# First layer's feed-forward output product by seven quarter products for 24 of its 32 inner tiles

## The chip, the cores and the metric

The kernel runs on one core of one Trainium2 chip. The metric is the time of one execution in microseconds; a lower time is better.

## The reference

The input x has 512 tokens of 1024 features, in float32. Two layers run one after the other, each of a mixer and a feed-forward part:

```python
h1 = layer_norm(ALPHA * x + mixer(x), ln1_g, ln1_b)          # ALPHA = 4 ** 0.25
ffn = square(relu(h1 @ w1 + b1)) @ w2 + b2                   # w1: 1024 x 4096, w2: 4096 x 1024
x = layer_norm(ALPHA * h1 + ffn, ln2_g, ln2_b)
```

The mixer of the first layer is a state-space scan beside a stick-breaking attention, that of the second layer a gated convolution over 31 tokens. The change lies in `square(...) @ w2` of the first layer.

## The kernel before

**Number format.** Each float32 operand of a product is split in two parts, hi (a cast by ScalarE) and lo (the operand minus hi, a subtraction on VectorE). A product of 128 inner rows takes three matmuls: hi x hi, hi x lo, lo x hi. This holds for weights and for activations. `gemm` (L258) issues them with 128x128 weights as the stationary operand and 512 or 256 tokens as the moving one, so results lie with features on partitions and tokens along the row.

**Stages** of the first layer, by the names in the trace: `tla` is the mixer's output product with its second half, `fl` the first six hidden tiles ("lead", computed while the layer norm `a` of the second half of the tokens runs), `f` the other hidden tiles, `acf` the output product into `X` (`accum`), `tlb` the output product of the last eight inner tiles, which runs half by half of the tokens into layer norm `b`. Then `pl`, `pv`, `pg` are the first product of the convolution. The 4096 inner features are 32 tiles of 128. The first layer takes them in four blocks of eight: eight `f` tiles, then 8 feature tiles x 8 inner tiles x 3 matmuls of `acf`; the last block's is `tlb`. So `acf` is 3 x 192 matmuls over 512 tokens.

**The second layer** takes its inner tiles in blocks of 6, 6, 6, 6 and 8, and uses Strassen's scheme in the form of Winograd (seven products of quarters in place of eight) for the first 24. The trace calls these products `s` (L1400). A block's activations are made by `pair`: two hidden tiles, each relu and square on ScalarE, then four sums of quarters on VectorE (`q`), then the split into `ah` and `al`. The weights' quarters lie in four buffers `quad`; `Weights.operand` makes the combinations in place by four subtractions (L133 to L139), and each of the seven operands is split to hi and lo (128x1536). `seven` has the activations stationary and 512 features moving, so its results lie by tokens.

**Weights** come through one list of units (`W.units`), in the order of their use. SP issues a load into a buffer `raw` (two of them), ScalarE casts it (L112), VectorE subtracts (L113), and the pair lands in a slot. `W.next()` hands out the next unit and prepares those ahead of it: five ahead over eight slots in the first layer, three ahead over four slots in the second layer's feed-forward. A slot can be filled again when what read it has ended.

**Kept weights.** 30 units of the second layer (24 of the convolution, the first six of its `w1`) are loaded and split during the first layer's feed-forward, and SP writes hi and lo back to memory (`kepth`, `keptl`, 512 KB each). POOL loads them later without a split. `keep_at` says behind which step each of them is handled.

**Memory.** Pools are stacks. `mw` has three slots, `w2` above it `raw` and five slots, `hid` at the other end the temporary tiles and the convolution's pages. When the second layer's feed-forward begins (`turn`), these pools are closed and smaller ones (slots `s1` to `s4`, `raw`, the activations `a0` to `a2`, `q`, `w` for the quads) are opened over the same bytes; a new tile waits for the old tiles under it. The order in which the engines get their instructions is made by a scheduler from dependencies and program order, so PE's matmuls need not come in program order.

Of the kernel before, what the change touches and what calls it, by code (L numbers as in the profile page):

```python
# [39 lines left out]
FFN_BLOCKS = ((8, 8, 8, 8), (6, 6, 6, 6, 8))  # L40
# [7 lines left out]
KEEP_FROM = 8  # L48
# [11 lines left out]
class Weights:  # L60


    def __init__(self, tc, ahead):
        self.tc, self.nc, self.ahead = tc, tc.nc, ahead
        self.slots, self.units, self.raw, self.urgent, self.fence, self.hold = [], [], None, True, None, False
        self.done, self.got, self.chunk, self.ready, self.kept = 0, 0, {}, {}, {}
        self.turn, self.quads, self.base = None, {}, 0
# [19 lines left out]
    def _prep(self, n):  # L87
        nc = self.nc
        while self.done < min(n, len(self.units)):
            key, src, nk, ncol, off, width = self.units[self.done]  # L90
            if self.turn and self.done == self.turn[0]:
                self.turn[1]()
# [106 lines left out]
def kernel(ctx: ExitStack, tc: tile.TileContext, a: dict, out: bass.AP):  # L199
# [7 lines left out]
    def const(shape, name, dt=F32):  # L207
        return cst.tile(shape, dt, tag=name, name=name)
# [4 lines left out]
    X = [const([P, T], f"X{j}") for j in range(KT)]  # L213
# [49 lines left out]
    wst = ExitStack()  # L263
    wpool = wst.enter_context(tc.tile_pool(name="mw", bufs=1))
# [600 lines left out]
    wp2 = wst.enter_context(tc.tile_pool(name="w2", bufs=1))  # L865
    hst = ExitStack()
    hid = hst.enter_context(tc.tile_pool(name="hid", bufs=1, side="right"))
# [11 lines left out]
    def hpage(name, dt=F32R, w=T):  # L879
        return hid.tile([P, PAD + T + 2], dt, tag="hid", name=name, bufs=16)[:, :w]  # L880

    def tmp(name, dt=F32):
        return hid.tile([P, T], dt, tag="tmp", name=name, bufs=8)
# [9 lines left out]
    later += units_of("pw2", a["conv_w_pw2"][0], 0, 8, range(0, D, 128), 256)  # L893
    later += units_of("f1l", a["ffn_w1"][1], 0, 8, range(0, LEAD * P, 128), 256)

    kept = [k for j in range(0, 16, 4) for k in (j, j + 2, j + 1, j + 3)] + list(range(16, 24 + LEAD))
    keep_at, n = {}, 0
    for layer in range(2):
        if layer:
            units += [(("split", i), None, 8, 128, 0, 0) for i in range(24 + LEAD)]  # L900
            at_turn = len(W.units) + len(units)
        k0 = 0
        for nb in FFN_BLOCKS[layer]:
            if layer:
                units += units_of("f11", a["ffn_w1"][1], 0, 8, range(max(k0, LEAD) * P, (k0 + nb) * P, 128), 128)
                if nb == NB:
                    units += [(("quad", k0, i), None, nb // 2, T, 0, 0) for i in ORDER7]
                else:
                    for c in (0, T):
                        for k, n_ in ((0, 3), (3, 3), (6, 2)):  # L910
                            src = a["ffn_w2"][1][(k0 + k) * P : (k0 + k + n_) * P, c : c + T].rearrange("(k p) n -> p k n", p=P)
                            units.append((("f21", k0 + k, c), src, n_, T, 0, T))
                k0 += nb
                continue
            for m in range(k0, k0 + nb, 4):
                units += units_of("f10", a["ffn_w1"][0], 0, 8, range(m * P, min(m + 4, k0 + nb) * P, 128), 256)
                if m >= KEEP_FROM:
                    keep_at["f", m + 3] = kept[n : n + 2]
                    units += [later[i] for i in kept[n : n + 2]]
                    n += 2  # L920
            for j in range(0, KT, 4):
                units += units_of("f20", a["ffn_w2"][0], k0, nb, range(j * P, (j + 4) * P, 128), 256)
                if k0 + nb < 32:
                    m = 4 if j else 2
                    keep_at["a", k0, j + 3] = kept[n : n + m]
                    units += [later[i] for i in kept[n : n + m]]
                    n += m
            k0 += nb
    W.add_slots(wp2, 5)
# [150 lines left out]
    def ffn1(layer, bi, k0, nb, xs, fps, first=()):  # L1080
        hs = []
        for i in range(nb):
            m = k0 + i
            if i < len(first):
                ps = first[i]
            else:
                ps = fps(f"f{layer}{m}")
                gemm(ps, W.next(), slice(0, P), xs, 0, T)
            r = tmp(f"fr{layer}{m}")
            act(r, ps, AF.Relu, bias=pv("ffn_b1", 32 * layer + m))  # L1090
            tt(r, r, r, ALU.mult)
            pg_ = page if (i < 4) == (bi % 2 == 0) else hpage
            hh, hl = pg_(f"hh{layer}{m}"), pg_(f"hl{layer}{m}")
            split(hh, hl, r)
            hs.append((hh, hl))
            for k in keep_at.get(("f", m), ()) if layer == 0 else ():
                W.keep(k)
        return hs


# [6 lines left out]
    xs, first = tail_norm_lead(cat[4:8], "a", rb[0], ("ln1_g", 0), ("ln1_b", 0), LEAD, "fl0")  # L1107
    wdw = hid.tile([P, KT, CONV], F32, tag="wdw", name="wdw")
    mask = hid.tile([P, 32], F32, tag="mask", name="mask")

# [11 lines left out]

    k0 = 0
    for bi, nb in enumerate(FFN_BLOCKS[0]):
        if bi == 1:
            taps()
        hs = ffn1(0, bi, k0, nb, xs, nps, first if bi == 0 else ())
        if bi < len(FFN_BLOCKS[0]) - 1:
            accum(nps, hs, f"f0{bi}", 1024 // nb, bi == 0, keep=lambda j: keep_at.get(("a", k0, j), ()))
        k0 += nb  # L1130
    xs, first = tail_norm_lead(hs, "b", rb[1], ("ln2_g", 0), ("ln2_b", 0), 4, "pl")
# [188 lines left out]
    f1 = {}  # L1320

    def turn():
        wst.close()
        hst.close()
        f1.update((x, ctx.enter_context(tc.tile_pool(name=f"f1{x}", bufs=1, reuse_waits="tile"))) for x in "s1 s2 raw s3 a1 s4 a2 a0 q b w".split())
        W.slots, W.base, W.raw, W.ahead = [], W.done, f1["raw"], NSLOT - 1
        for x in ("s1", "s2", "s3", "s4"):
            W.add_slots(f1[x], 1)
        W.quad = f1["w"]
        W.load_quads(0, a["ffn_w2"][1], 0, NB)  # L1330

    W.turn = (at_turn, turn)
# [4 lines left out]
    nb_last = FFN_BLOCKS[1][-1]  # L1337
# [13 lines left out]
    R1 = [page(f"R1{t}", F32) for t in range(2)]  # L1351

    def rect(m, ps):

        r = page(f"r1{m}", F32)
        act(r, ps, AF.Relu, bias=pv("ffn_b1", 32 + m))
        return r

    def hidden(m):

        ps = stp(f"f1{m}")
        gemm(ps, W.next(), slice(0, P), xs, 0, T)
        return ps

    def split_part(hi, lo, src):
        S.copy(hi, src)
        V.tensor_sub(lo, src, hi.bitcast(F32))

    def pair(m, pss):

        q = f1["q"].tile([P, 8, H], F32, tag="q", name=f"q{m}", bufs=2)
        hi, lo = (f1[f"a{m // 2 % 3}"].tile([P, 7, H], F32R, tag=f"a{x}", name=f"a{x}{m}", bufs=1) for x in "hl")
        for e in range(2):
            r = rect(m + e, pss[e] if pss else hidden(m + e)).rearrange("p (h c) -> p h c", h=2)
            act(q[:, 1:3] if e else q[:, 0:8:7], r, AF.Square)
        split_part(hi[:, 0:3], lo[:, 0:3], q[:, 0:3])
        tt(q[:, 3], q[:, 7], q[:, 2], ALU.add)
        tt(q[:, 4], q[:, 3], q[:, 0], ALU.subtract)
        tt(q[:, 5], q[:, 0], q[:, 7], ALU.subtract)
        tt(q[:, 6], q[:, 1], q[:, 4], ALU.subtract)  # L1380
        split_part(hi[:, 3:7], lo[:, 3:7], q[:, 3:7])
        return hi, lo

    PLACE = {1: 0, 2: 1, 4: 2, 5: 3, 6: 4, 7: 5, 3: 6}

    def seven(blk, As, first):

        bank = {}
        for i in ORDER7:
            wh, wl = W.next()  # L1390
            chain = {3: 5, 7: 6, 4: 6}.get(i, i)
# [22 lines left out]
    for bi, nb in enumerate(FFN_BLOCKS[1][:-1]):  # L1414
        if bi:
            W.load_quads(k0, a["ffn_w2"][1], k0, nb)
        As = [pair(m, first[m : m + 2] if bi == 0 else None) for m in range(k0, k0 + nb, 2)]
        if bi == 0:
            residual()
        seven(k0, As, bi == 0)  # L1420
        k0 += nb
    hs = []
    for i in range(nb_last):
        if i % 3 == 0:
            hl_ = [f1[f"a{i // 3}"].tile([P, 3, T], F32R, tag=f"a{x}", name=f"b{x}{i}", bufs=1) for x in "hl"]
        r = rect(k0 + i, hidden(k0 + i))
# [88 lines left out]
```

## Time and profile before

| | |
|---|---|
| median of 3 runs (lowest, highest) | 1165.17 us (1160.34, 1166.05) |
| profiled execution | 1164.9 us |
| its span, first to last instruction | 1163.2 us |
| granted TensorE clock | 0.994 |
| PE busy | 1133.7 us, 97% |
| DVE (VectorE) busy | 820.6 us, 71% |
| ACT (ScalarE) busy | 550.0 us, 47% |

Durations below come from the profiled execution. A matmul's recorded duration overlaps with the next one's, so the rate of matmuls is read from the length of an unbroken stretch divided by its count. "DMA share" is the mean busy share of the core's 16 DMA engines.

### The profile page before, as it was taken

What the parts mean: (1) busy time and instruction counts of PE and PEld (TensorE: products, weight loads), DVE (VectorE), ACT (ScalarE), POOL (GpSimd) and SP (SyncE); (2) the same over time, 40 slices, a digit from 0 to 9 for tenths busy, and PEclk for the clock granted to TensorE, in tenths of its full rate; (3) what the DMA queues carried; (4) which work ended last, traced back from release to release, by engine and by line L of the source; (5) the groups of instructions that cost most, each with busy time, mean ns of one, the idle gap of its engine ahead of it and who ended that gap; (6) DMA issues with size and microseconds to landing.
All of it is one profiled execution on the core that took longest, in us unless ns stands there. A gap on an engine that the chain in (4) does not pass through costs nothing.

```text
span 1163.2 us, 17835 instructions
## 1 busy us (share of the span) xinstructions
PE 1133.7 (97%) x7156; PEld 948.5 (82%) x7156; DVE 820.6 (71%) x1401; ACT 550.0 (47%) x838; POOL 70.2 (6%) x125
## 2 busy tenths in 40 slices
PE   9989989999999999999999999999999999999997
PEld 7777767799888888888899867689988888888885
DVE  7999865578645645645647699988695958588337
ACT  7857759435524524523513231364673536263530
POOL 1022221000000000000002211002000000000000
PEclk9999989999999999999999999999999999999999
DMA  9621212150878778788617634156024151515211
GB/s 204 173 63 50 74 56 74 55 181 14 267 244 289 250 273 282 267 268 274 217 46 245 226 137 146 39 170 227 4 82 135 50 151 44 172 35 156 65 54 73
DMA packets 145907, 169.59 MB, mean 146 GB/s; under 512 B 13922, under 2 KB 119138, under 8 KB 145824
## 3 DMA queue, kind: packets, MB, share of 16 engines
q1 hardware_dynamic: 137024, 136.96, 37.1%
q0 software_dynamic: 8640, 31.46, 8.0%
q8 instruction: 56, 0.92, 0.3%
q14 instruction: 27, 0.22, 0.1%
q10 hardware_dynamic: 160, 0.03, 0.0%
HBM read 132.12 MB, written 35.65 MB: 144 GB/s over the span
## 4 chain that ended last, share of the span: by engine, by line
PE 78%; DMA 6%; DVE 6%; ACT 5%; issue 2%; SPq 2%; POOL 1%; DVEq 0%; ACTq 0%
PE f L258 20%; PE acf L258 10%; PE s L1400 10%; DMA raw<-in_ffn_w_dram 4%; PE tld L258 4%; PE h L1445 4%; PE tlb L258 4%; PE fl L258 3%; PE pv L258 3%; PE cw L1174 3%; PE pg L258 3%; PE tla L258 2%; PE acmo L258 2%; DVE wlo L113 2%; PE pl L258 2%
## 5 line engine op out<-in xcount | busy, mean ns | idle before, releaser
L112 ACT CAST whi<-raw 128x1024 fp32r<-128x1024 f32 (+1 forms) x150 | 156.6, 1061 | 259.1 <-PE acf L258 66.3
L113 DVE TENSOR_TENSOR wlo<-raw,whi 128x1024 fp32r<-128x1024 f32 (+1 forms) x150 | 183.6, 1236 | 122.1 <-ACT whi L112 122.1
L258 PE MATMUL f<-xah,whi 128*128 128x512 f32 x208 | 81.0, 390 | 0.0
L258 PE MATMUL f<-xal,whi 128*128 128x512 f32 x208 | 81.0, 389 | 0.0
L258 PE MATMUL f<-xah,wlo 128*128 128x512 f32 x208 | 80.9, 389 | 0.0
L258 PE MATMUL f<-xdh,whi 128*128 128x512 f32 x208 | 80.9, 389 | 0.0
L258 PE MATMUL f<-xdl,whi 128*128 128x512 f32 x208 | 80.9, 389 | 0.0
L258 PE MATMUL f<-xdh,wlo 128*128 128x512 f32 x208 | 80.9, 389 | 0.0
L258 PE MATMUL acf<-hl,whi 128*128 128x512 f32 x192 | 75.8, 395 | 0.1
L258 PE MATMUL acf<-hh,wlo 128*128 128x512 f32 x192 | 75.7, 394 | 0.0
L258 PE MATMUL acf<-hh,whi 128*128 128x512 f32 x192 | 75.3, 392 | 0.0
L1400 PE MATMUL s<-whi,al 128*128 128x512 f32 x168 | 65.0, 390 | 0.0
L1400 PE MATMUL s<-wlo,ah 128*128 128x512 f32 x168 | 64.9, 390 | 0.0
L1400 PE MATMUL s<-whi,ah 128*128 128x512 f32 x168 | 64.5, 392 | 0.0
L113 DVE TENSOR_TENSOR wlo<-quad,whi 128x1536 fp32r<-128x1536 f32 x28 | 49.1, 1754 | 7.6 <-ACT whi L112 7.5
L391 DVE SCALAR_TENSOR_TENSOR cy<-hp,wdw,cy 128x512 f32<-128x512 f32 (+1 forms) x75 | 49.5, 660 | 0.5 <-ACT cy L187 0.5
L112 ACT CAST whi<-quad 128x1536 fp32r<-128x1536 f32 x28 | 41.0, 1483 | 17.2 <-PE f L258 8.0
L97 POOL DMA_DIRECT2D whi<-kepth x30 | 16.0, 535 | 547.6 <-PE tlb L258 386.7
L258 PEld LDWEIGHTS f<-xdh,whi 128*128 128x128 f32 x208 | 39.0, 188 | 8.1
L258 PEld LDWEIGHTS f<-xah,wlo 128*128 128x128 f32 x208 | 39.0, 188 | 8.1
L258 PEld LDWEIGHTS f<-xah,whi 128*128 128x128 f32 x208 | 39.0, 188 | 8.1
L258 PEld LDWEIGHTS f<-xdl,whi 128*128 128x128 f32 x208 | 39.0, 188 | 8.1
(647 smaller groups left out, 3064.4 us busy)
## 6 DMA issues: line engine op xcount, KB each, us to landing
raw<-in_ffn_w_dram SPq DMA_DIRECT2D x35, 1024.0 KB, 6.0
kepth<-whi SPq DMA_DIRECT2D x30, 512.0 KB, 4.4
keptl<-wlo SPq DMA_DIRECT2D x30, 512.0 KB, 9.5
whi<-kepth POOLq DMA_DIRECT2D x30, 512.0 KB, 3.6
wlo<-keptl POOLq DMA_DIRECT2D x30, 512.0 KB, 4.4
raw<-in_ffn_w_dram SPq DMA_DIRECT2D x28, 512.0 KB, 4.0
raw<-in_conv_w_pw_dram SPq DMA_DIRECT2D x12, 1024.0 KB, 6.7
quad<-in_ffn_w_dram SPq DMA_DIRECT2D x16, 768.0 KB, 4.6
```

Source lines behind the costliest of these rows:

```text
L97: nc.gpsimd.dma_start(x, d)
L112: i0 = nc.scalar.copy(hi, raw).ins
L113: i1 = nc.vector.tensor_sub(lo, raw, hi.bitcast(F32)).ins
L258: ins = PE.matmul(ps[:, c0:c1], u[:, k, ksl], v[:, c0:c1], start=start and k == 0 and i == 0, stop=stop and k == n - 1 and i == 2).ins
L391: V.scalar_tensor_tensor(o, x, s, y, op0=op0, op1=op1)
L1174: PE.matmul(cps[j, c0][g][C, :], Ds[j][t // 16][R, t % 16, :], hps[j][R, t + c0 : t + c1], start=t < 4, stop=t >= n - 4, tile_position=(R. ...
L1400: PE.matmul(ps, u, v[:, p, :], start=chain == i and p == 0 and n_ == 0, stop=p == len(As) - 1 and n_ == 2, skip_group_check=True)
L1445: PE.matmul(ps, u, v, start=k == 0 and i == 0, stop=k == nb_last - 1 and i == 2)
```

## The change

The first layer takes the block sizes of the second (6, 6, 6, 6, 8) and the quarter products for its first 24 inner tiles. `quad` loads, `operand`, `pair` and the weight slots are those of the second layer, now functions of the layer. What is new is `seven_by_feature`: the weights stay stationary and the moving operand is a quarter of the activations, 256 tokens, so that results stay by features. Products 2, 5, 6, 3, 7, 4 are added to regions of `X` (which is now one tile, so that two feature tiles are added in one instruction), product 1 is gathered in two pages `R1` and added to `X` in the last block. `X` is scaled by ALPHA, and its bias added, by eight ScalarE instructions ahead of the blocks.

Pools change three times, not once: to the small ones at the end of the first layer's lead (`quarters(0)`), back to eight slots, `raw` and `hid` at the end of the fourth block (`plain`), and again to the small ones in the second layer (`quarters(1)`). The 30 kept units are loaded one by one (512 KB) where two came in one load (1024 KB), and so are the hidden weights of blocks 1 to 3. Their places: three in block 0's products, three among the hidden tiles and four among the products of each of blocks 1 to 3, six in the last block. The second layer's feed-forward computes as before.

```diff
-FFN_BLOCKS = ((8, 8, 8, 8), (6, 6, 6, 6, 8))
+FFN_BLOCKS = (6, 6, 6, 6, 8)
-KEEP_FROM = 8
+KEEP_AT = ((0, 3, 6), (0, 2, 4, 6), 6)
...
-        later += units_of("pw1", a["conv_w_pw1"][0], 0, 8, [j], 256)
-        later += units_of("pw1", a["conv_w_pw1"][0], 0, 8, [D + j], 256)
+        later += [units_of("pw1", a["conv_w_pw1"][0], 0, 8, [c], 128)[0] for c in (j, D + j)]
...
+        for bi, nb in enumerate(FFN_BLOCKS[:-1]):
+            for m in range(k0, k0 + nb, 2):
+                f1_units(m, 2)
+                if bi:
+                    kept("f", m)
+            for n, i in enumerate(ORDER7):
+                units.append((("quad", k0, i), None, nb // 2, T, 0, 0))
+                if n in KEEP_AT[bi > 0]:
+                    kept("p", k0, n)
...
+            turn_at.append(len(W.units) + len(units))
+            for m in range(k0, k0 + nb, 2):
+                units += units_of("f10", w1, 0, 8, range(m * P, (m + 2) * P, 128), 256)
+                if m - k0 < kept_last:
+                    kept("l", m)
+                    kept("l", m + 1)
+            units += units_of("f20", w2, k0, nb, range(0, D, 128), 256)
...
+    def quarters(layer):
+        def turn():
+            wst[0].close()
+            wst[0] = ExitStack()
+            f1.update((x, wst[0].enter_context(tc.tile_pool(name=f"f1{layer}{x}", bufs=1, reuse_waits="tile")))
+                      for x in "s1 s2 raw s3 a1 s4 a2 a0 q b w".split())
+            W.slots, W.base, W.raw, W.ahead = [], W.done, f1["raw"], NSLOT - 1
...
+    def plain():
+        wst[0].close()
+        wst[0] = ExitStack()
+        p1, p2 = (wst[0].enter_context(tc.tile_pool(name=x, bufs=1, reuse_waits="tile")) for x in ("mw2", "w22"))
+        hid[0] = wst[0].enter_context(tc.tile_pool(name="hid2", bufs=1, side="right", reuse_waits="tile"))
+        W.slots, W.base, W.raw, W.ahead = [], W.done, p2, 5
+        W.add_slots(p1, 3)
+        W.add_slots(p2, 5)
+
+    W.turns = {turn_at[0]: quarters(0), turn_at[1]: plain, turn_at[2]: quarters(1)}
...
-    xs, first = tail_norm_lead(cat[4:8], "a", rb[0], ("ln1_g", 0), ("ln1_b", 0), LEAD, "fl0")
+    xs, first = tail_norm_lead(cat[4:8], "a", rb[0], ("ln1_g", 0), ("ln1_b", 0), LEAD, "fl0", None, 3)
+    for j in range(KT):
+        act(X[j], X[j], AF.Identity, bias=rb[1][:, j : j + 1], scale=ALPHA)
...
+    def seven_by_feature(k0, As, first):
+        bank, opened = {}, None
+        for n, i in enumerate(ORDER7):
+            wh, wl = W.next()
+            chain = CHAIN.get(i, i)
+            for b in range(2):
+                if chain == i:
+                    bank[i, b] = nps(f"z{k0}{i}{b}")
+                ps = bank[chain, b]
+                for d in range(2):
+                    c = slice((2 * b + d) * P, (2 * b + d + 1) * P)
+                    for p, (ah, al) in enumerate(As):
+                        uh, ul = ah[:, PLACE[i]], al[:, PLACE[i]]
+                        for n_, (u, v) in enumerate(((wh, uh), (wh, ul), (wl, uh))):
...
+                            opens = chain == i and p == 0 and n_ == 0
+                            ins = PE.matmul(ps[:, d * H : (d + 1) * H], u[:, p, c], v, start=opens and d == 0,
+                                            stop=p == len(As) - 1 and n_ == 2, skip_group_check=True).ins
...
+            for b in range(2):
+                ps = bank[chain, b]
+                if i == 1:
+                    if first:
+                        S.copy(R1[b], ps)
+                    else:
+                        tt(R1[b], R1[b], ps, ALU.add)
+                else:
+                    x = region({2: 0, 5: 3, 6: 1, 3: 1, 7: 3, 4: 2}[i], b)
+                    tt(x, x, halves(ps), ALU.add)
+            if ("p", k0, n) in keep_at:
+                W.keep(keep_at["p", k0, n])
...
     for bi, nb in enumerate(FFN_BLOCKS[:-1]):
+        if bi:
+            W.load_quads(k0, a["ffn_w2"][0], k0, nb)
+        As = [pair(0, m, xs, first[m : m + 2] if bi == 0 else None) for m in range(k0, k0 + nb, 2)]
+        seven_by_feature(k0, As, bi == 0)
         k0 += nb
+    W.prep_to(W.got + 1)
...
+    hs = []
+    for i in range(FFN_BLOCKS[-1]):
+        m = k0 + i
+        ps = nps(f"f0{m}")
+        gemm(ps, W.next(), slice(0, P), xs, 0, T)
...
+        x = region(i // 2, i % 2)
+        tt(x, x, halves(R1[i % 2]), ALU.add)
...
-    xs, first = tail_norm_lead(hs, "b", rb[1], ("ln2_g", 0), ("ln2_b", 0), 4, "pl")
+    xs, first = tail_norm_lead(hs, "b", None, ("ln2_g", 0), ("ln2_b", 0), 4, "pl")
```

More of the change, by code (lines that the diff above doesn't have):

```diff
@@ L899 @@
         if layer:
             units += [(("split", i), None, 8, 128, 0, 0) for i in range(24 + LEAD)]
[L901 to L927, printed above, removed]
-            k0 += nb
@@ L1349, in residual @@
                 S.copy(X[4 * f + b], pss[b])
[L1351 to L1384, printed above, removed]
+    R1 = [page(f"R1{t}1", F32) for t in range(2)]
     def seven(blk, As, first):
```

156 lines of the change are left out of this document (98 added, 58 removed).

## The prediction

> **What bounds the kernel now.** I read the page's engine table first, then the waits of PE, the chain that ended last, and the stretches of both feed-forwards.
>
> ```profile
> span 1163.2 us, 17835 instructions
> PE 1133.7 (97%) x7156; PEld 948.5 (82%) x7156; DVE 820.6 (71%) x1401; ACT 550.0 (47%) x838; POOL 70.2 (6%) x125
> ...
> PE tlb L258 <- ACT hh L248: 0.9, 1, 0.9
> ...
> 317.88 39.71 PE acf L258 x170
> 358.19 43.75 PE f L258 x192
> 401.94 44.59 PE acf L258 x192
> 446.53 43.52 PE f L258 x192
> 490.05 32.98 PE acf L258 x143
> ...
> 614.32 11.42 PE tlb L258 x96
> 625.73 2.88 PE pl L258 x24
> ...
> 851.26 3.65 PE xt L1346 x32
> 854.92 28.71 PE s L1400 x126
> 883.63 32.64 PE f L258 x144
> 916.27 28.85 PE s L1400 x126
> ```
>
> PE works 97% of the span, and from `acf` to `tlb` its only listed wait is 0.9 us. The pieces of the chain (start, length, what) abut, so a matmul taken from here shortens the run, and any gap made here lengthens it. The rate is length by count: 0.2267 us for 512 tokens in `f` (43.52/192), 0.2322 in `acf` (117.28/505 over its three pieces), 0.1200 and 0.1190 for 256 tokens in `pl` and `tlb`. Half the tokens cost more than half.
>
> ```profile
> core 0: us, PE busy (x) PEld busy (x) DVE busy (x) ACT busy (x) POOL busy (x), PEclk, DMA share, GB/s
> 357.60:401.94 44.34, 44.34 (x201) 36.78 (x202) 27.89 (x33) 22.99 (x30) 0.00 (x0) 1.00 0.83 285
> 301.50:582.00 280.50, 279.84 (x1240) 229.26 (x1238) 152.50 (x169) 116.33 (x138) 0.00 (x0) 1.00 0.78 266
> 883.63:916.27 32.64, 32.64 (x145) 27.03 (x145) 21.20 (x23) 16.95 (x20) 0.00 (x0) 1.00 0.21 61
> 916.27:945.11 28.84, 28.84 (x127) 23.50 (x127) 24.48 (x27) 12.06 (x12) 0.00 (x0) 1.00 0.51 150
> ```
>
> Behind PE stand the DMA engines in the first layer (78% over 280.5 us, with the kept weights) and DVE in the second layer's products (24.48 of 28.84 us). The change brings both into one place.
>
> **The matmuls.** Removed: 3 x 192 = 576 of `acf`, 576 x 0.2322 = 133.8 us. Added: 4 blocks x 7 products x 4 feature tiles x 3 pairs' inner tiles x 3 = 1008 over 256 tokens, x 0.1200 = 121.0 us. So **-12.8 us**; with equal cost per column it would have been 576 x 0.125 x 0.2322 = 16.7. The `f` tiles and the last block's `tlb` keep their counts.
>
> On the full-speed rate the Trainium skill (TensorE: Matmul & The Clock Gate, Back-to-back issue gap) has N/2.4 + 2.5 ns, an estimate of 215.8 and 109.2 ns here; the two products would then differ by 14.2 us. The rows above are 5% to 10% longer, and the measurement decides.
>
> **VectorE and ScalarE.**
>
> ```profile
> L113 DVE TENSOR_TENSOR wlo<-raw,whi 128x1024 fp32r<-128x1024 f32 x146 | 176.6, 1222 | 107.2 <-ACT whi L112 107.1
> L112 ACT CAST whi<-raw 128x1024 fp32r<-128x1024 f32 x146 | 150.7, 1049 | 248.3 <-PE acf L258 66.3 <-PE s L1400 46.7 <-PE f L258 44.6
> L113 DVE TENSOR_TENSOR wlo<-quad,whi 128x1536 fp32r<-128x1536 f32 x28 | 49.1, 1754 | 7.6 <-ACT whi L112 7.5
> L112 ACT CAST whi<-quad 128x1536 fp32r<-128x1536 f32 x28 | 41.0, 1483 | 17.2 <-PE f L258 8.0 <-PE s L1400 7.3 <-PE fl L1058 1.8
> L387 DVE TENSOR_TENSOR X<-X,s 128x512 f32<-128x512 f32 x48 | 31.9, 682 | 11.9 <-PE s L1400 11.9
> L1367 DVE TENSOR_TENSOR al<-q,ah 128x768 fp32r<-128x768 f32 x12 | 11.5, 955 | 0.1
> L187 ACT ACTIVATE X<-X,rb 128x512 f32<-128x512 f32 x16 | 10.2, 719 | 0.0
> ```
>
> The second layer's rows carry every operation of a new block: four subtractions and seven splits of quads, three pairs, 14 additions of 512 columns. To them come 3 kept splits among the hidden tiles and 4 among the products, 1.222 us of DVE and 1.049 of ACT each. Products: 24.48 + 4 x 1.222 = 29.4 us of DVE in 252 x 0.1200 = 30.2 us of PE. Hidden tiles: 21.20 + 3.7 = 24.9 of 32.64. DVE fits, at 97% in the products. ACT has 12.06 + 4.2 of 30.2 there. The square moves from DVE to ACT, the eight scalings of `X` (5.8 us of ACT) are needed only at the second product's addition: nothing, while ACT has this room. The eight additions of `R1` (5.5 us of DVE) lie beside the last block's 43.5 us of `f`: nothing.
>
> **Hidden tiles to products.** At this passage the last pair isn't ready.
>
> ```profile
> 916.30 0.69 ACT L187 ACTIVATE r<-f,PV 128x512 f32<-128x512 f32 x1 [2.15 <-PE f L258]
> 917.02 0.63 ACT L187 ACTIVATE q<-r 128x512 f32<-128x512 f32 x1
> ...
> 918.93 0.83 ACT L1366 CAST ah<-q 128x768 fp32r<-128x768 f32 x1
> ```
>
> Its `ah` comes 3.5 us after `s` began, though program order wants it after six matmuls (1.4 us). PE went on with other pairs and lost 28.85 - 126 x 0.2267 = 0.3 us. In the new ring of four slots the last hidden tile's slot is next filled by product 2 (second layer: product 6): cast and subtraction, 1.483 + 1.754 = 3.2 us, against 36 x 0.12 = 4.3 us of product 1. At best 0, at worst the whole 3.2 us for each of three blocks. I take 0.3 each, **+0.9**, because the nearest rows show it; in the products themselves the slots are given back late (rivals).
>
> **First change of pools.** The leads lie in the old slots 4, 5, 6, 7, 0, 1 (units 28 to 33 over eight). `s1` covers slots 0 and half of 1, so product 1's lo waits for the last lead.
>
> ```profile
> 839.30 1.47 ACT L112 CAST whi<-quad 128x1536 fp32r<-128x1536 f32 x1 [1.80 <-PE fl L1058]
> ...
> L258 PE MATMUL fl<-xah,wlo x96: 278/283/467, 264.9 to 301.5; 128*128 128x256 f32 x96
> ```
>
> The second layer shows such a wait of a quad's cast for a lead. Here the leads end at 301.5, lo is there 1.754 us later; product 2 (slot `s3`) and the hi parts are free earlier, and two of three pairs are done. The last pair also starts at 301.5: 0.69 + 0.63 on ACT, 0.83 of cast, 0.955 on DVE, 3.1 us before its first part is there, 1.754 more if DVE takes product 1's lo first. So between 0 and 4.9 us; I take **+1.0**, since PE reorders but has no transposes (3.65 us of `xt`) to put there.
>
> **Second change (`plain`).** Counting units, the fourth block's product 4 lies in `s1`, under the new slot 0. The first `f` tile of the last block can be cast only when the last matmul of that block has ended: 1.049 for hi, 1.222 for lo. Lower end 1.05 (hi suffices for two thirds of its matmuls), upper 2.3 plus signals. **+2.3**: lo is the third matmul.
>
> **Staging in the last block.**
>
> ```profile
> raw<-in_ffn_w_dram SPq DMA_DIRECT2D x35, 1024.0 KB, 6.0
> kepth<-whi SPq DMA_DIRECT2D x30, 512.0 KB, 4.4
> keptl<-wlo SPq DMA_DIRECT2D x30, 512.0 KB, 9.5
> ...
> raw<-in_ffn_w_dram SPq DMA_DIRECT2D x28, 512.0 KB, 4.0
> ...
> ACT whi L112 <- DMA raw<-in_ffn_w_dram: 33.8, 19, 5.5
> ```
>
> Two `f` tiles (10.9 us of PE) bring one load of 1024 KB, two of 512 KB, four writes of 512 KB: 4.2 MB, three times. At the rate that 285 GB/s at a share of 0.83 gives (343) that is 12.2 us. Lower end 0 (loads begun under the products), upper 3 x (4.2 MB / 290 - 10.9) = 10.8, with 290 from 61 at 0.21. I take **+1.5**, about one of the three excesses at 343.
>
> The Trainium skill (DMA: Bandwidth & Descriptors, Anatomy of one DMA) puts a fixed 2.0 us on each transfer, so two halves of a load cost one such more. The rows agree: 2 x 4.0 against 6.0. By it the 24 split loads carry 48 us of added latency, spread over two buffers; it speaks against the change, in the second rival.
>
> **SP's queue.** A block's four quad loads wait for buffers that are freed by the casts of products 6, 3, 7 and 4; behind them stand the next hidden weights and the kept writes.
>
> ```profile
> 921.24 12.01 SPq L126 DMA_DIRECT2D quad<-in_ffn_w_dram  x4
> ...
> 935.21 23.29 SPq L78 DMA_DIRECT2D raw<-in_ffn_w_dram  x6
> ```
>
> In the second layer the queue stands 12 us on them, from 921 on, and PE, with three units prepared, shows no gap. The first layer adds two kept writes for each kept unit to the same queue; a write that is held back holds a slot. I put nothing here and leave it to the rivals. POOL's queue gets nothing new.
>
> **Third change.** The second layer's leads move by the new count to slots 6, 7, 0, 1, 2, 3: the first two quad casts, at 836.04 and 839.30 now, wait for leads 3 and 4, some 6 to 9 us later, with `xt` and DVE's queue behind. From 0 to 3.5 us (two DVE splits); **+0.5**, as `s` begins only at 854.92.
>
> None of these terms can fall below nothing: PE has no gap in `acf` and `f` that they could close.
>
> **Sum**: -12.8 + 0.9 + 1.0 + 2.3 + 1.5 + 0.5 = **-6.6 us**. The profiled execution took 1164.9 (span 1163.2 and 1.7 around), 0.3 below the median of 1165.17: forecast **1158.3**.
>
> **Rivals.**
>
> *All is hidden.* PE reorders as it does at 916, loads come ahead; only the 1.05 us of `plain` remains: -11.7, 1153.2. For it: no gap at three such passages of the second layer. Against: there the DMA share is 0.5, here above 0.8.
>
> *The transfers become the bound* (the other side). A block moves 3.1 MB of quads, 3.1 of hidden weights, 3.7 of kept loads and 7.3 of kept writes, 17.3 MB in 62.9 us: 275 GB/s, a share of 0.80 at 343, 0.95 at 290. Among the hidden tiles, if the quads fall there, 11 MB in 32.6 us want 337: at 290 it is 37.9, +5.3 in each of three blocks. With 10.8 in the last block, and half of these 16: -6.6 - 1.5 + 10.8 + 8 = +10.7, 1175.6. It decides from 14 us lost. For it: casts already wait 33.8 us for loads here. Against: PE showed no gap at 285.
>
> *The ring of four slots.* A kept unit holds its slot for 1.0 + 1.2 us of split and 9.5 of `keptl`, near 12 us or three products; product 7's lo, refilled behind the kept unit cast after product 1, comes at 4.3 + 12 + 1.8 = 18 us, wanted at 21.6. With DVE at 97% its queue can eat these 3.5 us. At 2 us a block: -6.6 - 0.9 + 8 = +0.5, 1165.4, no change.
>
> **Chances.** Forecast (1154.5 to 1161): 0.35; all hidden 0.20; slots 0.28; transfers 0.17. A measurement tells 0.5% (5.8 us) from no change, so faster means below 1159.3: 0.28 of the forecast's, the 0.20, and 0.02 of the slots': 0.50. Slower, above 1171: 0.15, of the transfers. Within: 0.35, the rest of each. The range reaches from 1152, all of the matmuls' gain, over the slots' case to 1171 and leaves out the transfers' 0.15 above that.
>
> **What would show it.** `z` matmuls 0.120 apart, 121 us in all (first step); PE gaps at the leads' end, at each passage from `f` to `z`, about 2.3 us at the end of the fourth block, and at the second layer's first `s`; the DMA share above 0.83, and `f` of the last block waiting for `whi`. It is wrong if `z` runs slower than `pl`, or if PE's waits on `whi` and `wlo` in the first layer pass 14 us.

## The result and the profile after

The changed kernel takes 1197.04 us (median of 4 runs, 1193.13 to 1200.89) against 1163.14 (1160.34 to 1166.05): a ratio of 1.0291 (95% interval 1.0237 to 1.0345). It is slower, and far outside the predicted range. The profiled execution took 1193.67 us, 28.8 more than that of before.

First the page of the changed kernel: span, engines, and the clock by slices.

```profile
span 1191.8 us, 18891 instructions
PE 1137.0 (95%) x7588; PEld 971.6 (82%) x7588; DVE 893.6 (75%) x1475; ACT 599.3 (50%) x884; POOL 66.7 (6%) x125
...
PEclk9999999999899999987999999999999999999999
```

PE's recorded busy time hardly moves, yet its share falls to 95%; the clock row, in tenths, dips in the middle of the run. Next stretches of the changed kernel, with the columns of before: the first layer's feed-forward, all behind it, and the products of one block from their first gap on.

```profile
298.47:654.43 355.96, 327.55 (x2032) 296.17 (x2031) 253.69 (x307) 167.78 (x193) 7.57 (x14) 0.95 0.69 226
654.43:1191.00 536.57, 525.23 (x3856) 439.18 (x3855) 404.00 (x652) 232.40 (x345) 24.34 (x46) 1.00 0.34 110
...
440.00:475.00 35.00, 30.87 (x243) 30.17 (x242) 30.85 (x32) 15.03 (x15) 0.00 (x0) 0.95 0.74 244
```

From the start of the last `fl` matmul to the first `pl` ("the stretch" below) it is 355.9 us, and was 324.0 (301.54 to 625.57). From there to the end both kernels take 537.6. So all of the loss lies in the stretch: PE works 327.55 of 355.96 us of it, at a mean clock of 0.95. The DMA share is 0.69 (0.74 in the same stretch of before). That is a mean, and it doesn't show whether the transfers bind at single places.

I took the stretch apart by the start times of its matmuls. An interval beyond 0.120 us (256 tokens) or 0.227 (512; `acf` at its own 0.232) is a gap; inside the windows in which the granted clock is 0.50, the excess is put to the clock.

| us | before | after |
|---|---|---|
| `acf` / `z`, at full rate | 133.4 | 121.0 |
| `f`, `tlb` and rest, at full rate | 188.5 | 188.3 |
| gaps | 2.1 | 34.7 |
| halved clock | 0 | 11.9 |

So the matmuls give 12.4 us, and gaps (+32.6) and clock (+11.9) take more than three times that. The gaps by place: end of the leads and block 0, 2.0 + 0.5 + 3.7 = 6.2; the three passages from `f` to `z` 3.5, 4.7 and 5.1, together 13.3; the end of the fourth block 10.0; the rest of the last block 3.0; small ones the remainder. The chain of the changed kernel holds the pieces between them (start, length, what, count):

```profile
337.97 21.57 PE f L259 x95
...
449.65 16.95 PE z L1200 x139
```

An unbroken piece of `z` (L1200 is `seven_by_feature`'s matmul) takes 16.95/139 = 0.122 us each, one of `f` 0.227. What PE waited for, in the waits of the changed kernel (us in total, times, longest):

```profile
PE z L1200 <- DVE wlo L113: 7.9, 4, 3.5
PE z L1200 <- ACT whi L112: 7.4, 4, 3.6
PE wd L1169 <- DMA wn<-in_conv_w_dw_dram: 5.2, 2, 4.2
PE f L259 <- ACT whi L112: 4.6, 2, 3.3
PE z L1200 <- DVE al L1107: 2.2, 4, 1.2
...
PE s L1469 <- ACT X L1451: 0.7, 1, 0.7
```

Split weights come late (L112 the cast, L113 the subtraction), and the taps' load `wn` once, at the turn. A passage in the timeline of the changed kernel (start, length, instruction, in brackets the idle time before it and its releaser):

```profile
506.02 1.06 ACT L112 CAST whi<-raw 128x1024 fp32r<-128x1024 f32 x1 [2.61 <-DMA raw<-in_conv_w_pw_dram]
506.98 0.68 ACT L187 ACTIVATE r<-f,PV 128x512 f32<-128x512 f32 x1
508.66 1.47 ACT L112 CAST whi<-quad 128x1536 fp32r<-128x1536 f32 x1 [1.00 <-DMA kepth<-whi]
510.04 1.04 ACT L1106 CAST ah<-q 128x1024 fp32r<-128x1024 f32 x1
510.99 0.63 ACT L187 ACTIVATE q<-r 128x512 f32<-128x512 f32 x1
511.52 1.46 ACT L112 CAST whi<-quad 128x1536 fp32r<-128x1536 f32 x1
...
513.03 0.38 PE L1200 MATMUL z<-ah,whi 128*128 128x256 f32 x1 [3.59 <-ACT whi L112]
```

ACT stands 2.61 us on the load of a kept unit (a convolution weight, of no use to this layer) and 1.00 us until a write-back has freed a slot. What stands behind on its in-order queue, the pair's operations and the next product's cast, is late by that, and PE waits 3.59 us. SP's issues of the changed kernel (KB each, median us to landing) show the write-backs quicker than before, when `keptl` took 9.5 us, but `keptl` still outlasts a product of 36 x 0.120 = 4.3 us:

```profile
kepth<-whi SPq DMA_DIRECT2D x30, 512.0 KB, 3.6
keptl<-wlo SPq DMA_DIRECT2D x30, 512.0 KB, 5.4
```

And the turn to the last block, in the same timeline:

```profile
545.34 0.26 SPq L1166 DMA_DIRECT2D wn<-in_conv_w_dw_dram  x1
545.70 1.02 SPq L78 DMA_DIRECT2D raw<-in_ffn_w_dram  x2
...
550.24 0.63 PE L1169 MATMUL wd<-ident,wn 31*128 31x31 f32 x4 [4.21 <-DMA wn<-in_conv_w_dw_dram]
...
553.10 2.94 ACT L112 CAST whi<-raw 128x1024 fp32r<-128x1024 f32 x3 [14.74 <-DMA raw<-in_ffn_w_dram]
554.20 0.80 PE L259 MATMUL f<-xah,whi 128*128 128x512 f32 x1 [3.33 <-ACT whi L112]
```

The taps (`wn`, L1166) go to a page of `hid2`, which exists only after the fourth block; SP waited 5.3 us with that load, until 545.3, and the hidden weights of the last block (L78) were queued behind it. PE stood 4.21 us on the taps' little transposes and 3.33 us on the first cast.

### The profile page after: what moved, and what is told of

Its sections match the earlier page's. It is cut to its first block, busy times and chain, and to the rows that moved or that the text cites. A ratio compares the mean times of both kernels' runs of the same rounds, so it can differ in the third digit from the quotient of the medians.

```text
span 1191.8 us, 18891 instructions
## 1 busy us (share of the span) xinstructions
PE 1137.0 (95%) x7588; PEld 971.6 (82%) x7588; DVE 893.6 (75%) x1475; ACT 599.3 (50%) x884; POOL 66.7 (6%) x125
## 4 chain that ended last, share of the span: by engine, by line
PE 63%; DVE 10%; DMA 8%; ACT 6%; issue 1%; SPq 0%; POOL 0%; DVEq 0%; ACTq 0%
PE f L259 15%; PE s L1469 10%; PE z L1200 7%; PE fl L259 5%; PE tld L259 4%; PE h L1514 4%; PE tlb L259 4%; DVE wlo L113 3%; DMA raw<-in_ffn_w_dram 3%; ACT whi L112 2%; PE tla L259 2%; PE pv L259 2%; PE acmo L259 2%; DMA keptl<-wlo 2%; DVE cy L393 2%; PE pl L259 2%
## 5 line engine op out<-in xcount | busy, mean ns | idle before, releaser
L113 DVE TENSOR_TENSOR wlo<-raw,whi 128x1024 fp32r<-128x1024 f32 (+1 forms) x126 | 155.2, 1240 | 129.1 <-ACT whi L112 126.9
L112 ACT CAST whi<-raw 128x1024 fp32r<-128x1024 f32 (+1 forms) x126 | 133.0, 1065 | 235.5 <-DMA raw<-in_ffn_w_dram 81.4
L112 ACT CAST whi<-quad 128x1536 fp32r<-128x1536 f32 x56 | 82.3, 1481 | 49.4 <-PE z L1200 15.9
L113 DVE TENSOR_TENSOR wlo<-quad,whi 128x1536 fp32r<-128x1536 f32 x56 | 98.0, 1754 | 10.3 <-ACT whi L112 5.8
L1200 PE MATMUL z<-ah,wlo 128*128 128x256 f32 x336 | 97.2, 294 | 7.9 <-DVE wlo L113 7.9
L1200 PE MATMUL z<-ah,whi 128*128 128x256 f32 x336 | 96.6, 295 | 7.4 <-ACT whi L112 7.4
L1200 PE MATMUL z<-al,whi 128*128 128x256 f32 x336 | 97.7, 293 | 2.2 <-DVE al L1107 2.2
L1200 PEld LDWEIGHTS z<-ah,wlo 128*128 128x128 f32 x336 | 67.2, 202 | 8.9 <-DVE wlo L113 8.9
L1200 PEld LDWEIGHTS z<-ah,whi 128*128 128x128 f32 x336 | 67.0, 203 | 8.5 <-ACT whi L112 8.2
L1200 PEld LDWEIGHTS z<-al,whi 128*128 128x128 f32 x336 | 67.2, 200 | 3.5 <-DVE al L1107 3.4
L1106 ACT CAST ah<-q 128x768 fp32r<-128x768 f32 (+1 forms) x48 | 45.1, 945 | 35.3 <-DVE q L389 33.9
L1107 DVE TENSOR_TENSOR al<-q,ah 128x768 fp32r<-128x768 f32 (+1 forms) x48 | 52.0, 1088 | 10.1 <-ACT ah L1106 10.0
L259 PEld LDWEIGHTS f<-xah,whi 128*128 128x128 f32 x208 | 40.0, 192 | 13.3 <-ACT whi L112 5.2
```

What stands on the lines that cost most here:

```text
L112: i0 = nc.scalar.copy(hi, raw).ins
L113: i1 = nc.vector.tensor_sub(lo, raw, hi.bitcast(F32)).ins
L259: ins = PE.matmul(ps[:, c0:c1], u[:, k, ksl], v[:, c0:c1], start=start and k == 0 and i == 0, stop=stop and k == n - 1 and i == 2).ins
L1200: ins = PE.matmul(ps[:, d * H : (d + 1) * H], u[:, p, c], v, start=opens and d == 0, stop=p == len(As) - 1 and n_ == 2, skip_group_check=T ...
```

## The experiments

My theory: the kept units make the passages late, above all because a slot is held until its write-back has landed; and the taps' load makes the turn late. There are two rivals: the pairs' operations and the weights' splits stand behind each other on the in-order queues of ACT and DVE, whose total work is too close to PE's, whoever holds the slots; and the transfers themselves are in each other's way.

All are judged by the stretch of one profiled execution beside the median, since the end of the leads itself varied. It lies at 297.7 to 299.4 us in the changed kernel and in e1 to e4, and at 301.5 to 308.5 in the seven kernels that have the taps ahead of it (301.5 before, 298.1 in e6_before_none). So the stretch may leave out a part of what the earlier taps cost. "Ratio" is to the kernel before on the same chip.

| | median us | ratio (95%) | stretch | gaps | halved clock |
|---|---|---|---|---|---|
| before | 1163.14 | | 324.0 | 2.1 | 0 |
| after | 1197.04 | 1.0291 (1.0237 to 1.0345) | 355.9 | 34.7 | 11.9 |
| e1_no_kept | 1173.60 | 1.0078 (1.0034 to 1.0122) | 335.6 | 19.6 | 6.7 |
| e2_no_store | 1182.44 | 1.0147 (1.0079 to 1.0215) | 342.0 | 25.4 | 6.8 |
| e4_store_elsewhere | 1188.18 | 1.0196 (1.0140 to 1.0253) | 348.5 | 31.1 | 7.8 |
| e6_before_none | 1162.54 | 0.9994 (0.9969 to 1.0019) | 323.2 | 1.3 | 0 |
| e3_taps_late | 1190.09 | 1.0213 (1.0158 to 1.0267) | 353.4 | 33.0 | 11.0 |
| e7_taps_early | 1190.17 | 1.0235 (1.0161 to 1.0309) | 346.8 | 31.0 | 7.2 |
| e5_none_early | 1164.59 | 1.0033 (1.0009 to 1.0057) | 323.4 | 12.0 | 2.9 |
| e8_kept_apart | 1193.89 | 1.0267 (1.0188 to 1.0346) | 351.0 | 31.4 | 10.9 |
| e9_pair_first | 1190.73 | 1.0235 (1.0162 to 1.0307) | 347.6 | 27.2 | 11.7 |
| e11_pool_order | 1188.80 | 1.0218 (1.0144 to 1.0292) | 343.8 | 27.1 | 7.7 |
| e12_kept_mid | 1186.24 | 1.0196 (1.0086 to 1.0306) | 342.8 | 27.9 | 5.8 |
| e11_none_ordered | 1164.84 | 1.0014 (0.9990 to 1.0039) | 320.2 | 11.7 | 0 |

**What the kept units cost.** e1_no_kept has no kept unit in the first layer; the second layer fills those slots from the unsplit weights.

```diff
-                keep_at[at] = i
-                units.append(later[i])
+                W.kept[i] = (later[i][1], later[i][1])
```

> The changed kernel without the 30 kept units in the first layer: they are neither loaded, split nor written back there, and the second layer fills those slots straight from the unsplit weights (so its results are left wrong, its matmuls the same). Theory A (a kept unit sits in the ring of four slots until its write-back has landed, and the casts of the next products stand behind it in order): the gaps at the passages from hidden tiles to products, 4 to 5 us each with the halved clock behind them, shrink to under 1 us; what remains is the change of pools at the fourth block's end. The first layer's stretch (last lead matmul to first pl) falls from 354 to about 330. Theory B (VectorE's work at the passage, quads and the last pair's sums, is too much by itself): the gaps at the passages stay at 3 us or more, stretch 345. Theory C (the transfers' rate is the bound): the stretch falls too, to about 330, and the experiments without and with the stores tell it from A.

The stretch falls by 20.3 us, the median by 23.4; 335.6 is above the 330 or so that theory A expected. The waits of e1_no_kept:

```profile
PE wd L1168 <- DMA wn<-in_conv_w_dw_dram: 5.5, 2, 4.5
PE f L259 <- ACT whi L112: 3.4, 1, 3.4
...
PE z L1199 <- DVE al L1106: 2.6, 3, 0.9
PE z L1199 <- ACT whi L112: 2.4, 3, 0.9
```

The wait on `wlo` is gone from the list's head, the passages of blocks 1 to 3 cost 1.0 us each, and the turn is as it was (4.5 and 3.4 us). So the kept units are what makes the passages late, and not the turn.

e2_no_store loads and splits the kept units and writes only the first back; e4_store_elsewhere writes as many bytes, from pages that hold other data and in four transfers a unit where there were two, so that no slot waits for a write.

```diff
 # e2
+        if self.kept:
+            self.kept[i] = self.kept[0]
+            return
 # e4
-        for x, d in zip(w, self.kept[i]):
-            self.nc.sync.dma_start(d, x.bitcast(F32))
+        for e, d in enumerate(self.kept[i]):
+            for h in range(2):
+                src = self.other[2 * h + e][0].bitcast(F32).rearrange("p (k n) -> p k n", n=P)
+                self.nc.sync.dma_start(d[:, 4 * h : 4 * h + 4, :], src)
...
+    W.other = xs
```

> The changed kernel with all 30 kept units loaded and split, but only the first written back (the second layer reads that one each time; its results are wrong for it). Slots are free after the split. Theory A: passages' gaps under 1.5 us, stretch about 335. Theory B: gaps stay at 3 to 4 us each, since the splits on VectorE stay, stretch 348 or more. Theory C: stretch about 335 too.

> The changed kernel with the same 30 kept units and as many bytes written back, but from the layer's input pages in place of the slots (results of the second layer are wrong for it), so that a slot isn't held by a write-back. Theory A: stretch about 335 to 340, as without stores. Theory C: as in the changed kernel, about 352, since the bytes are the same. Theory B: about 352.

By the stretches, holding slots costs 355.9 - 348.5 = 7.4 us, the writes themselves 6.5, loads and splits 6.4: three parts of like size. By the medians they are 8.9, 5.7 and 8.8. Each part rests on one profiled execution and two to four times of a kernel, and the changed kernel's own times spread over 7.8 us, so the order of the three isn't shown. Both measures put the held slots and the writes together (13.9 of 20.3 us by the stretches) above the loads and splits. The held slots alone are not the main part as I had it.

The gaps in the products of blocks 1 to 3, small ones included, are plainer: 14.7 us in the changed kernel, 11.9 in e4, 6.3 in e2 and 4.1 in e1. In e2 VectorE is busy 252.5 us of the stretch, as in the changed kernel (253.7), since every split is still made. So loads and splits cost 2.2 of these 10.6 us, and the rest goes with the write-backs. The DMA share ahead of a passage, twice in the changed kernel and once in e2 (a transfer counts in the stretch in which it begins, so a share can pass 1):

```profile
436.00:440.00 4.00, 4.00 (x24) 3.49 (x23) 3.35 (x4) 3.74 (x4) 0.00 (x0) 1.00 1.02 366
505.00:509.20 4.20, 4.20 (x26) 3.69 (x24) 4.00 (x5) 2.18 (x3) 0.00 (x0) 1.00 1.02 350
...
436.00:441.00 5.00, 4.40 (x32) 3.74 (x31) 4.97 (x5) 3.53 (x5) 0.00 (x0) 1.00 0.09 28
```

The mean of 0.69 hides that the DMA engines are full just there. Whether the writes act through the transfer rate or through SP's queue, these runs don't part.

e6_before_none takes the kept units out of the kernel before, whose second layer then fills from the unsplit weights.

```diff
-                    keep_at["f", m + 3] = kept[n : n + 2]
-                    units += [later[i] for i in kept[n : n + 2]]
...
-                        keep_at["a", k0, j + 3] = kept[n : n + m]
-                        units += [later[i] for i in kept[n : n + m]]
...
+    for i, u in enumerate(later):
+        W.kept[i] = (u[1][:, :, u[4] : u[4] + 128],) * 2
```

> The kernel before without the kept units in the first layer (the second layer fills from the unsplit weights, its results are left wrong). Theory A (eight slots with five ahead hide the kept units): the first layer's stretch stays at 322 to 324 us, where the changed kernel lost 20 us by them. Rival (the kept units cost the kernel before as well): 315 or less.

The first layer's stretch of e6_before_none:

```profile
298.13:621.30 323.17, 322.89 (x1599) 272.26 (x1598) 143.52 (x201) 94.66 (x124) 12.40 (x14) 1.00 0.41 101
```

The DMA share falls from 0.74 to 0.41, and PE gains nothing: the same work was free in the kernel before, with eight slots, DVE at 54% and five units ahead, and costs 20 us in the changed one. Which of these conditions made it free was not tried one by one.

**The turn.** e3_taps_late moves `taps()` behind the last hidden tile; e7_taps_early moves it ahead of the leads, into a small pool of its own.

```diff
 # e7 (e3: the three lines of wdw, mask and taps() moved behind the loop over the last block's f)
+    tp = ctx.enter_context(tc.tile_pool(name="tp", bufs=1, side="right"))
...
+    wdw = tp.tile([P, KT, CONV], F32, tag="wdw", name="wdw")
+    mask = tp.tile([P, 32], F32, tag="mask", name="mask")
...
+    taps()
     xs, first = tail_norm_lead(cat[4:8], "a", rb[0], ("ln1_g", 0), ("ln1_b", 0), LEAD, "fl0", None, 3)
...
-    wdw = hid[0].tile([P, KT, CONV], F32, tag="wdw", name="wdw")
-    mask = hid[0].tile([P, 32], F32, tag="mask", name="mask")
-    taps()
```

> The changed kernel with the convolution's taps (two loads of 62 KB, eight transposes, the mask) moved from the change of pools behind the last block's eight hidden tiles. Theory D (the taps' load waits on the queue of SP for bytes that the fourth block's products still use, and the first two loads of the last block stand behind it): those loads are issued about 5 us sooner, the gap at the end of the fourth block falls from 4.4 + 1.7 us and a clock halved for 13.7 us to about 2.5 us without or with one short halving, total 8 to 14 us less than the changed kernel. Rival: those loads wait for their own bytes, and nothing moves beyond 2 us.

> The changed kernel with the taps made ahead of the first layer's tail, nothing else. Theory S (with the queue of SP free, the last block's loads are issued some 5 us sooner, but each two tiles still bring one load of 1024 KB and two kept ones of 512 KB through two buffers): the gap at the change of pools falls to about 2 us without a halved clock; gaps of 1 to 2 us come later in the last block. Stretch 346 to 350 against 355.9. Rival (taps alone): 342 or less.

Stretches of e3_taps_late: the turn, what follows it, and a later place of the same block.

```profile
546.40:549.60 3.20, 1.10 (x6) 0.47 (x4) 2.77 (x5) 2.00 (x2) 0.00 (x0) 1.00 0.61 164
549.60:560.00 10.40, 10.32 (x45) 8.56 (x46) 3.61 (x4) 3.91 (x5) 0.00 (x0) 1.00 0.76 227
573.00:576.30 3.30, 1.29 (x5) 0.48 (x3) 0.73 (x2) 1.76 (x2) 0.00 (x0) 1.00 0.92 287
576.30:583.10 6.80, 6.27 (x16) 4.84 (x16) 3.56 (x4) 3.87 (x6) 0.00 (x0) 0.50 0.80 241
```

The gaps of the turn fall from 10.0 to 2.6 us and the clock stays full behind it, so the taps' load is the cause of the turn's gaps; but PE then stops at 573, at a DMA share of 0.92 beside the kept units of the last block, and the clock halves there. Of the 7.4 us of gaps taken away at the turn, the stretch keeps 2.5; the median is 7.0 lower, under the 8 to 14 that theory D expected. e7 keeps 9.1 in the stretch, and its median is 6.9 lower; its leads end 5.5 us later than those of the changed kernel, so its profiled execution is only 3.6 us shorter.

**Both together.** e5_none_early is e1 with the taps early.

> No kept units in the first layer (as in the earlier experiment) and the taps made ahead of the first layer's tail, so that nothing of them lies at the change of pools. Theory: what is then left of the change is the matmuls' gain, 12.8 us, minus the two changes of pools. First layer's stretch about 322 us (335.6 less 4.7 + 3.5 + 1.5 us of gaps and half of a clock halved for 13.7 us, plus 2.5 for the first cast), and about 2 us under the kernel before without kept units. Rival (the taps weren't the cause at the change of pools; the loads of the last block wait for their own bytes): 333 or more.

Its stretch, 323.4, equals that of e6_before_none, 323.2; the median is 2.05 us above. With kept units and taps gone from the picture, the gain of the matmuls is still eaten by 12.0 us of gaps and 2.9 of halved clock. The gaps of blocks 1 to 3 are 1.0 each, of the leads' end and block 0 3.9, of the turn 2.4; the rest are under 0.5 each. The stretch came near the expected 322, but the run is not the 2 us shorter than e6 that was expected with it.

**Remedies.** e8_kept_apart is e7 with two slots for the kept units alone and three for all others (to find room, one `q` buffer, not two).

```diff
+            if self.apart and key[0] in ("pw1", "pw2", "f1l"):
+                pool, s = self.apart[self.nkept % len(self.apart)]
+                self.nkept += 1
+                self.base += 1
...
+            W.apart = [] if layer else [(f1["k1"], 8), (f1["k2"], 9)]
```

> As the run before it, and kept units have two slots of their own in blocks 0 to 3, beside three for the products and hidden weights (paid for by one buffer fewer of the pairs' squares). Theory A (the ring is held by write-backs): another 7 us less, as when the write-backs came from elsewhere, stretch about 340. Rival (the order on VectorE and ScalarE: the kept units' casts now wait for their own slots and stand ahead of the products' casts): no gain or a loss, 347 or more.

It gains nothing on e7 (351.0 against 346.8). Since it also has a slot and a `q` buffer less for the rest, it doesn't clear the slots of blame; it shows only that splitting the same memory in this way is no cure.

e9_pair_first is e7 with the pairs' operations of the first layer given precedence on their engines (`high_priority` around relu, square, sums and split).

> The run with the taps made early, and the pairs' relu, squares, sums and splits of the first layer given precedence over the weights' casts where both are ready. Theory O (at the passage the last pair's cast and split stand in the engines' order behind a quad's cast that itself waits for a subtraction or a write-back): gaps in z fall from 23 to about 12 us, stretch 346.8 to about 335. Rival A (the weights themselves come late, because their slots are held): gaps move from the pair's tiles to whi and wlo of the products, stretch 344 or more.

ACT at one passage of e9_pair_first, and two rows of its waits:

```profile
442.53 1.47 ACT L112 CAST whi<-quad 128x1536 fp32r<-128x1536 f32 x1 [1.25 <-DMA kepth<-whi]
...
448.97 1.48 ACT L112 CAST whi<-quad 128x1536 fp32r<-128x1536 f32 x1 [0.87 <-DVE quad L135]
```

```profile
PE z L1208 <- ACT whi L112: 8.8, 3, 3.6
PE z L1208 <- DVE wlo L113: 5.0, 3, 2.1
```

The gaps inside `z` fall from 23.1 to 15.6 us, but 1.8 us more at its first matmul and 4.5 more of halved clock take 6.3 of these 7.5 us back, and the stretch doesn't gain (347.6 against 346.8). PE's wait in `z` for the pairs' `al` falls from 4.1 us in e7 to 0.2, while its waits for the weights' casts and splits stay (14.4 us in e7, 13.8 here).

e11_pool_order is e9 with the small pools of the first change laid so that the first quads don't lie under the last leads (order `a2 s4 raw s1 s3 a1 s2 a0 q b w`). e12_kept_mid is e9 with kept units moved out of the passages:

```diff
-KEEP_AT = ((0, 3, 6), (0, 2, 4, 6), 6)
+KEEP_AT = ((2, 4, 5), (1, 2, 3, 4, 5), 6)
...
-                if bi:
+                if bi and m < k0 + 4:
```

> As the run with pairs first, kept units present, with that order of the small pools. Theory P: 3 to 7 us less than without it, by the gap of 2 us at the leads' end and the halved clock behind it. Rival: the kept units' write-backs (the second unit of that block is one) keep the first passage late, less than 2 us.

> As the run with pairs first, and kept units moved away from the passages: two a block among the hidden tiles instead of three (none behind the last pair), five among the products 2 to 7 instead of four from product 1 on. Theory A (a kept unit ahead of a passage holds the slot of the first products): gaps at the passages fall by 2 us each, stretch 5 to 8 us less than with pairs first. Rival B (VectorE's load among the products, 24.5 + 5 x 1.2 = 30.6 us of 30.2): gaps appear inside the products, no gain or a loss.

In e11_pool_order the gap from `fl` to `z` is gone, but the gaps in all stay (27.1 us against 27.2): the 3.8 us that the stretch gains on e9 are halved clock, 7.7 us against 11.7. In e12_kept_mid the gaps in `z` fall to 13.7 and those in `f` rise to 11.0, and the sum is 27.9; its 4.8 us are halved clock too (5.8). So neither remedy shortens the waits; they fall at other places. Both intervals of the ratio lie above 1.

e11_none_ordered is e11_pool_order without kept units (the second layer fills from the unsplit weights), the best that these remedies leave.

> No kept units in the first layer, taps early, pairs first, and the small pools of the first change in another order (the last pair's tiles a2 and the fourth slot over the leads' last bytes, the first slot over bytes that are free), so that product 1 needn't wait for the last leads. Theory P (the first passage is late because slot s1 lies under the leads 4 and 5): gap at the leads' end 1.0 us to 0, the two halvings of the clock there gone, stretch 323.4 to about 316, the matmuls' gain all but reached. Rival (the activations are late there, not the weights): 320 or more.

Its stretch:

```profile
307.15:627.34 320.19, 312.35 (x2023) 285.00 (x2022) 221.07 (x276) 138.18 (x163) 12.38 (x14) 1.00 0.41 99
```

The stretch is 320.2 us, at full clock throughout, 3.0 below e6_before_none and above the 316 that theory P expected. Against e5 the gaps stay (11.7 and 12.0 us), and the halved clock goes. The leads end at 307.2 us, 9.0 later than in e6, and the median is not below the kernel before (interval 0.9990 to 1.0039). No version beats the kernel before.

## Why the prediction was wrong, step by step

The forecast was -6.6 us, and the stretch grew by 31.9: 38.5 us apart. The kept units make 20.3 of it (e1), the taps at the turn 12.2 more once the kept units are gone (335.6 - 323.4, e5), and 6.0 remain in e5, whose stretch is 0.6 us below that of the kernel before in place of 6.6.

**The matmuls: right.** `z` takes 121.0 us at full rate, its median interval 0.120, as `pl` said. The Trainium skill's formula (TensorE: Matmul & The Clock Gate, Back-to-back issue gap), which that section gives for isolated matmuls, is by the prediction's estimate 0.109, 9% below it; the row was the better source.

**The kept units beside the quads, priced at nothing: this step failed.** The prediction put nothing for VectorE and ScalarE ("DVE fits, at 97%") and nothing for the kept writes ("I put nothing here and leave it to the rivals"). Together they cost 20.3 us of the stretch. The writes and the slots that they hold make 13.9 of it, the loads and splits 6.4. The sum of work was near: at 440 to 475 DVE is busy 30.85 us where 29.4 were forecast for the products. What failed is the step from that sum to no waits. A share of 97% is an average over a block's products, while a passage needs its pair, its quad and its kept split within a few us, on in-order queues, and just there the DMA share is 1.02. The prediction had both the share and the cover ("while ACT has this room") and didn't name what is late when one cast waits for a write or a load. VectorE's load alone doesn't explain it: e2 has the same splits without the writes, and loses only 2.2 us more than e1 in the products of blocks 1 to 3.

**Hidden tiles to products, +0.9: mis-sized.** 13.3 us of gaps in place of 0.9. Without kept units it is 3 x 1.0 (e1): near the estimate, with the cause named there, the last pair's activations. The kept units make the rest, their write-backs above all (e2, e4).

**First change, +1.0 (0 to 4.9): mis-sized.** 6.2 us; without kept units 3.9 (e1), inside the bounds. The layout makes the gap from `fl` to `z` (zero in e11_pool_order), but another layout only moves it: in e11_none_ordered block 0 has gaps of 0.4, 1.5 and 1.8 us, 3.7 in all, where e5 had 3.9.

**Second change, +2.3: right in itself, and missing its queue.** Measured 10.0. With the taps away the gaps at the turn are 1.3 + 1.0 = 2.3 in e11_none_ordered, 2.4 in e5 and 2.6 in e3. Here the second failed step is the nothing put for SP's queue: the change moves the allocation of `hid2` to the end of the fourth block, so the taps' load waits for it, with the last block's weights behind. The prediction listed the quads and kept writes on that queue and not the taps.

**Staging in the last block, +1.5 (0 to 10.8): inside its bounds.** 3.0, and more where the turn is shorter (4.1 at 576 in e7).

**Third change, +0.5:** nothing net, 537.6 us in both kernels; `s` waited 0.7.

**Halved clock, not in the sum:** 11.9 us.

**Rivals.** The ring of four slots had the right mechanism in kind (a kept unit holds its slot until its write has landed, and DVE's queue eats the slack), priced at 2 us for each of four blocks. Holding slots costs 7.4, close to that 8, but partly by luck: `keptl` lands in 5.4 and not 9.5, and the writes, loads and splits of the same units cost 13 more. The transfers' rival had the right side, and its mechanism stays open. It wanted a share of 0.80 to 0.95 over a block, and the mean fell to 0.69; but ahead of the passages at 440 and 509 us the share is 1.02, and without the writes (e2) most of the gaps there are gone. The prediction's own test, PE's waits on `whi` and `wlo` above 14 us, came true: 7.9 + 7.4 + 4.6 = 19.9.

## What to carry to other kernels

Work that is free beside one arrangement has to be priced again beside the next: here 30 staged units cost nothing under long products with eight slots, and 20 us with four slots beside the quads' work. A share over a block, of an engine or of the DMA engines, says little about its passages; go through the in-order queue there, instruction by instruction, and ask what each one waits for. When a buffer's allocation moves, list every load that goes into it and what is queued behind that load.

## Of the hardware: short gaps and a halved clock

Before, the granted clock is full throughout the stretch. After, it fell to 0.50 six times, for 3.4, 6.8 or 13.7 us. Stretches of the changed kernel, two gaps and what follows them:

```profile
509.20:513.00 3.80, 0.24 (x2) 0.03 (x1) 2.83 (x3) 3.80 (x5) 0.00 (x0) 1.00 0.98 329
514.40:521.20 6.80, 5.76 (x26) 5.23 (x25) 6.80 (x7) 2.21 (x2) 0.00 (x0) 0.50 0.01 4
521.20:541.20 20.00, 20.00 (x169) 20.00 (x169) 18.88 (x23) 8.54 (x7) 0.00 (x0) 1.00 0.48 173
...
548.50:555.30 6.80, 1.73 (x6) 1.00 (x6) 1.41 (x2) 2.20 (x3) 0.00 (x0) 0.50 0.63 186
555.30:562.10 6.80, 5.80 (x16) 4.24 (x16) 2.66 (x4) 0.91 (x2) 0.00 (x0) 0.50 0.76 217
562.10:570.00 7.90, 7.90 (x36) 6.47 (x36) 4.01 (x4) 4.73 (x6) 0.00 (x0) 1.00 0.95 326
```

After 3.8 us of standing PE ran on for 1.4 us at full clock, then at half of it for 6.8: 26 matmuls where 57 fit, with one more gap of 1.2 us among them. So behind the gap of 3.8 us some 2.5 us more (6.8 - 26 x 0.120 - 1.2) went to the clock. The Trainium skill (TensorE: Matmul & The Clock Gate, Part 1) has the clock decided over free-running windows of 3413 ns, and the lengths here are one, two and four of them. The same page (Why this matters for your kernels) warns of idle gaps beyond about 3 us; in e1_no_kept gaps of 1.0 and 0.8 us, 1.6 us apart, were followed by 3.4 us at half clock, while in e11_none_ordered 1.3 and 1.0 us, 1.7 apart, were not. What decides between these was not tried; a position against the windows would fit.
